# A hybrid decoder layer on one NeuronCore: the inverse's reads on SyncE's queue, and five small moves of sums, groups and input

## The chip, the cores and the metric

The kernel runs on one core of a Trainium2 chip. The metric is the device time of one execution in microseconds, as the median of several runs. The engines are TensorE (PE), VectorE (DVE), ScalarE (ACT), GpSimd (POOL) and SyncE (SP); SP only issues DMAs here.

## What is computed

One layer over 272 positions (16 learned ones ahead of 256) and 2048 features, in float32, batch 1:

```
h = layer_norm(concat([meta, x]))
p = h @ w_in                                   # columns for two head groups
y_rwkv = rwkv7_mixer(p[..., :RWKV_COLS])       # 16 heads, delta-rule state of 64x64 each
y_sb = stick_breaking_mixer(p[..., RWKV_COLS:])    # 16 heads, causal, 128-query blocks
h = layer_norm(ALPHA * h + concat([y_rwkv, y_sb]) @ w_out)
h = layer_norm(ALPHA * h + conv_ffn(h))        # gated MLP, 5632 wide, causal convolution of 3
return h[:, 16:]
```

In the first mixer every position updates the state of its head: `S = S * dec + sa (kk a)^T + v k^T` with `sa = S (-kk)`, where `kk` is the key, scaled and divided by its norm over the head, and `y = S r`. The decay and the rate `a` come from low-rank products (`w2`, `a2`), a gate from `g2`.

## The kernel before

**Weights.** All weights come in pieces of 512 KB, 128 rows by 1024 columns at a time, in the order of use. `weight` (L160) loads a piece through SP's queue (L174) into one of three raw buffers, ACT rounds it to a high half (`whi`, L183), DVE forms the difference (`wlo`, L186), and PE makes three passes over each 128 columns: high by high, high by low, low by high. `passes` (L225) and `each_pass` (L477) are these. A raw buffer is free again when DVE's difference is done, so a load waits on SP for the difference of the piece three before it.

**Order.** PE's order is the program's (`manual_schedule`, L420). The order of the instructions on every other engine, and of the DMAs in each engine's queue, is written by a planner when the program is built: it places what it believes to be ready first by durations of its own, with priorities where the program gives them (L182, L682). Each engine then takes its list in order, and waits at the head of it until that instruction's inputs are there.

**Projection and mixers.** `ORDER` names the sixteen pairs of heads, R0 to R7 for the first mixer and S0 to S7 for the second; for each the three projections are made (48 passes each), and between them, after every 16 passes (`SLOT`), `slot` gives a turn to the tasks that are due. A task is a generator that yields how many slots it waits, and how many of two small PSUM banks (`BANKS`) it needs for its next step. For each pair of the first mixer `rwkv_front` begins when k is there (key norm: squares, sums `ss` over each head by PE, root and products), and `rwkv_back` when r is there: products of two decayed factors (AG, BK), then `gram`, 36 small matmuls, masked by DVE into AG (L623), stored by POOL to a DRAM scratch `dl` (L628) and read back by POOL as LT (L631).

**The inverse.** After every second pair, `inverse` (L663) solves 36 triangular systems of 32 on POOL: 31 steps of a product (L670) and a sum (L672). POOL then stores the result to a DRAM scratch `dy` (L673) and reads it back from there with twelve DMAs into TT, with rows and columns rearranged (L678). There are four inverses, one for each two pairs of heads. `chain` (L684) walks the nine blocks of 32 positions with TT: a product with the state, copied to Wt (L701) by DVE, a product with TT (L706), a product that updates the state (L718), with 16 passes of other work between them. `rwkv_post` (L753) normalises its result (sums `gnv`, by L536 and L537).

**The head.** The input is loaded as 16 rows (256 to 271) and two tiles of 128 rows, each of these in four DMAs (L308), all on SP; statistics and normalisation are on DVE for the tiles that don't begin at row 0, on ACT for the other one (L338 to L345). In the first projections, `lora` (L391) makes the low-rank products in eight groups of two products and two sigmoids, and a tail; `proj` (L271) makes R0's v in 16 steps of three passes and yields after every second one.

**The post-norm.** After w_out, POOL adds up the tiles and their squares (`gather`, L962). The gated MLP's first products `up_step` (L1021, three passes each) start before the norm is known; after step number `MEAN` of them PE makes the two sums `p1` and `p2` (L1038), and DVE and ACT form the factors (`vv`, `rn`, `mr`), with which the first four product tiles are settled (L1045) and the tiles normalised.

Of the kernel before, what the change touches and what calls it, by code (L numbers as in the profile page):

```python
# [12 lines left out]
ALU = mybir.AluOpType  # L13
PSUM = bass.MemoryType.PSUM

P = 128
D = 2048
KT = D // P
META = 16
SEQ = 256  # L20
T = META + SEQ
# [4 lines left out]
CH = 32  # L26
# [8 lines left out]
SLOT = 16  # L35
INVERSE = 18
UNITS = 16
MEAN = 8
LATER = 8
AHEAD = 300  # L40
WARM = 42
# [8 lines left out]
RG = 3  # L50
# [63 lines left out]
def hybrid_layer(ctx, tc, xin, cst, pvec, w2a2, g2, ln2, w_in, w_out, w_up, w_down, out, dbg=None):  # L114
    nc = tc.nc
    V, S, G, PE = nc.vector, nc.scalar, nc.gpsimd, nc.tensor
# [43 lines left out]
    def weight(i, ahead=None):  # L160
        if ahead is None:
            ahead = min(5 if extra else 3, max(0, first["up"] + 3 - i) if i < first["up"] else 5)
        while len(ready) < min(len(pieces), i + ahead + 1):
            n = len(ready)
            src, m = pieces[n]
            wide = int(np.prod(src.shape)) // P
            pl, bufs = (wp, HLB)
            if extra and n % 3 == 2:
                pl, bufs = (extra[0], 2)
            if n < 4 * 3:  # L170
                raw = xw.tile([P, wide], F32, tag="xraw", bufs=4, name=f"xraw{n}")
            else:
                raw = wp.tile([P, HALF], F32, tag="wraw", bufs=RAWB, name=f"wraw{n}")
            nc.sync.dma_start(raw[:, :wide].rearrange("p (m c) -> p m c", m=m), src)  # L174
            if n < 4 * 3:
                hi, lo = [xw.tile([P, wide], F32R, tag=t, bufs=6, name=f"{t}{n}") for t in ("xhi", "xlo")]
                S.copy(hi, raw[:, :wide])
                (G if n < 3 else V).tensor_tensor(out=lo, in0=raw[:, :wide], in1=hi.bitcast(F32), op=ALU.subtract)
                ready.append((hi, lo))
                continue  # L180
            hi = pl.tile([P, HALF], F32R, tag="whi", bufs=bufs, name=f"whi{n}")
            with tc.high_priority(offset=-LATER):  # L182
                S.copy(hi[:, :wide], raw[:, :wide])  # L183
            lo = pl.tile([P, HALF], F32R, tag="wlo", bufs=bufs, name=f"wlo{n}")
            with tc.high_priority(offset=-LATER):
                V.tensor_sub(lo[:, :wide], raw[:, :wide], hi[:, :wide].bitcast(F32))  # L186
            ready.append((hi, lo))
        return ready[i]
# [36 lines left out]
    def passes(ps, hi, lo, kk, xh, xl, start, stop):  # L225
        sl = slice(kk * P, kk * P + P)
        mm(ps, lhsT=hi[:, sl], rhs=xh, start=start, stop=False)  # L227
        mm(ps, lhsT=hi[:, sl], rhs=xl, start=False, stop=False)  # L228
        mm(ps, lhsT=lo[:, sl], rhs=xh, start=False, stop=stop)  # L229
# [11 lines left out]
    ht = [htile(F32R, f"h{kt}") for kt in range(KT)]  # L241
# [26 lines left out]
        n0 = max(n0, 1)  # L268
        V.scalar_tensor_tensor(dst[:, n0:T], ps[:, n0 - 1:T - 1], mu, dst[:, n0:T], op0=ALU.mult, op1=ALU.add)  # L269

    def proj(piece, ps, n0=0):  # L271

        for hf in range(2):
            hi, lo = weight(piece + hf)
            for kk in range(8):
                kt = hf * 8 + kk
                passes(ps[:, n0:T], hi, lo, kk, ht[kt][:, 0, n0:], ht[kt][:, 1, n0:], kt == 0, kt == KT - 1)
                if kk % 2:
                    yield


    sg = []
    order = ctx.enter_context(ExitStack())
    with ExitStack() as es:
# [19 lines left out]
        for n, (a, b) in enumerate(rows):  # L304
            xt = xp.tile([P, D], F32, name=f"xt{n}")
            for k in range(4 if n else 1):
                c = slice(k * 512, k * 512 + 512) if n else slice(0, D)
                nc.sync.dma_start(xt[:b - a, c], xin[a:b, c])  # L308
            xs.append((xt, b - a, a))
        nc.sync.dma_start(cc[:, :P], cst[:, :P])  # L310
        weight(2, ahead=0)
# [5 lines left out]
        for n, (xt, r, a) in enumerate(xs):  # L317
            mv, rs, mr = [xp.tile([P, w], F32, name=f"{m}{n}") for m, w in (("mv", 2), ("rs", 1), ("mr", 1))]
# [18 lines left out]
        def normalise(k):  # L337
            c = slice(k * 512, k * 512 + 512)  # L338
            for (xt, r, a), (mv, rs, mr) in zip(xs, norm):
                if a:  # L340
                    with tc.issue_after(last.ins):
                        V.tensor_scalar(out=xt[:r, c], in0=xt[:r, c], scalar1=mv[:r, 0:1], scalar2=rs[:r],
                                        op0=ALU.subtract, op1=ALU.mult)
                else:
                    S.activation(xt[:r, c], xt[:r, c], AF.Identity, scale=rs[:r], bias=mr[:r])  # L345
# [13 lines left out]
        for kt in range(KT):  # L359
# [4 lines left out]
            for m in range(3):  # L364
                hi, lo = weight(kt // 4 * 3 + m, ahead=3)
                n0 = 12 if m else 0
# [6 lines left out]
        o = PV["mu_r"][0]  # L373
# [47 lines left out]
        low = lora()  # L421
# [3 lines left out]
        shift(acc[3], 8, k_[:, PAD:])  # L425

        val = pst.tile([P, 512], F32, tag="acc", bufs=4, name="acc4")
        for n, _ in enumerate(proj(14, val)):
            next(low, None)
        for _ in low:  # L430
            pass
        shift(val, 16, v_[:, PAD:])
        tc.keep_in_program_order(nc.scalar.preload_act_table_set("natural_log_exp_and_others"))

# [7 lines left out]
    FULL, SQUARE, HALF_COLS, QUARTER_COLS = range(4)  # L442
# [63 lines left out]
    TT = [persistent(f"TT{p}", [P, NCH, 2 * CH]) for p in range(2)]  # L506
# [51 lines left out]
    def rwkv_front(j, st):  # L558

        a = sg[j][:, 1]  # L560
        sq = atile("sq", [P, TP])
        S.activation(sq, k_, AF.Square, scale=par("k_k", j))
        sq = halves(sq, "rn", "ss")
        cum = atile("cum", [P, TP])
        V.tensor_tensor_scan(out=cum, data0=reset, data1=sg[j][:, 0], initial=0.0, op0=ALU.mult, op1=ALU.add)
        S.activation(Pt[:, :, 1:], ch(cum), AF.Exp, scale=-DECAY)
        Pinv = cum
        S.activation(Pinv, cum, AF.Exp, scale=DECAY)
        yield 2, FULL, 1
        ps = misc("ss")  # L570
        by_head(ps[:, :TP], *sq)
        ss = atile("ss", [P, TP])
        V.tensor_scalar(out=ss, in0=ps[:, :TP], scalar1=16.0, scalar2=0.5e-24, op0=ALU.mult, op1=ALU.max)
        rn = atile("rn", [P, TP])
        S.activation(rn, ss, AF.Ln, scale=2.0 * KSC)
        S.activation(rn, rn, AF.Exp, scale=-0.5, bias=lnb[:, 1:2])
        y2 = atile("sq", [P, TP])
        S.activation(y2, rn, AF.Square)
        V.tensor_mul(ss, ss, y2)
        V.scalar_tensor_tensor(rn, ss, 1.5, rn, op0=ALU.subtract, op1=ALU.mult)  # L580
        kkn = rn
        V.scalar_tensor_tensor(kkn, k_, par("k_k", j), rn, op0=ALU.mult, op1=ALU.mult)
        ba = atile("ss", [P, TP])
        V.scalar_tensor_tensor(ba, kkn, -1.0, a, op0=ALU.mult, op1=ALU.mult)
        kp = st["kp"] = atile("kp", [P, TP])
        S.activation(kp, a, AF.Identity, scale=par("k_a", j), bias=omka[:, j:j + 1])
        give(f"sg{j}")
        V.tensor_mul(kp, kp, k_)
        BK = st["BK"] = wide(f"BK{j}", n=0).rearrange("p n t -> p (n t)").rearrange("p (c x t) -> p c x t", x=2, t=CH)
        V.tensor_mul(BK[:, :, 0], ch(ba), ch(Pinv))  # L590
        V.tensor_mul(BK[:, :, 1], ch(kp), ch(Pinv))
        st["kkn"] = kkn
# [70 lines left out]
    def inverse(q, LT, Y):  # L663

        tmp = atile("ytmp", [P, NR, CH])
        n_ = RG * NB
        for s in range(CH - 1):
            n = s // RG + 1
            m = CH - 1 - s
            G.tensor_tensor(out=tmp[:n_, :n, :m], in0=Y[:n_, :n, s:s + 1].to_broadcast([n_, n, m]),  # L670
                            in1=LT[:n_, s:s + 1, s + 1:].to_broadcast([n_, n, m]), op=ALU.mult)
            G.tensor_tensor(out=Y[:n_, :n, s + 1:], in0=Y[:n_, :n, s + 1:], in1=tmp[:n_, :n, :m], op=ALU.add)  # L672
        nc.gpsimd.dma_start(dy.rearrange("b (g r) t -> g b (r t)", g=RG), Y[:n_].rearrange("p r t -> p (r t)"))  # L673
        for n in range(4):
            x, o = n % 2, n * CH
            for g in range(RG):
                k = len(range(g, CH, RG))
                nc.gpsimd.dma_start(TT[q % 2][o + g:o + CH:RG, :, CH - x * CH:2 * CH - x * CH],  # L678
                                    dy[n * NCH:n * NCH + NCH, g * NR:g * NR + k].rearrange("c r t -> r c t"))

    def first_of_all():
# [189 lines left out]
    piece = 16  # L871
    state = [dict() for _ in range(NPAIR)]
    for kind, j in ORDER:
        st = state[j]
        if kind == "R":
            for n, dst in ((1, k_), (2, v_), (0, r_)):
                if n == 0 or j:
                    ps = bank(f"R{j}{n}")
# [7 lines left out]
        else:  # L886
            qkv = []
            for n in range(3):
                n0 = Q0 if n == 0 else 0
                ps = bank(f"S{j}{n}")  # L890
# [13 lines left out]
    hs, xt = [], []  # L904
# [11 lines left out]
    for i in range(EARLY):  # L916
        ps = bank(f"o{i}")
        weave(begun(i, ps))
        hs.append(htile(F32, f"x{i}"))
        x = hs[i][:, 0, :NQ]  # L920
        hi, lo = residual(i)
# [56 lines left out]
    for i in range(EARLY):  # L978
        hi, lo = weight(wi + i // 2)
        ps = bank(f"o{i}b")  # L980
# [9 lines left out]
    for i in range(EARLY, KT):  # L990
        ps = bank(f"o{i}")
        for hf in range(2):
            hi, lo = weight(wi)
            wi += 1
            for kk in range(8):
                n = hf * 8 + kk
# [7 lines left out]
        x = hs[i][:, 0, :NQ]  # L1004
        hi, lo = residual(i)
# [85 lines left out]
    for i in range(KT):  # L1091
        x = xt[i]
# [31 lines left out]
    for f in range(4, NF):  # L1124
        pair = []
        for m in range(2):
            ps = bank(f"u{2 * f + m}")
            for hf in range(2):
                hi, lo = weight(wi)
                wi += 1  # L1130
                for kk in range(8):
                    kt = hf * 8 + kk
# [146 lines left out]
```

## Time and profile before

| | |
|---|---|
| median of 3 runs | 1409.79 us (1408.15 to 1414.41) |
| the profiled execution's own time, and its span | 1412.04 us, 1410.3 us |
| mean granted TensorE clock | 0.971 of full speed |
| busy: PE, DVE, ACT, POOL | 1336.0, 943.1, 729.5, 251.9 us |
| DMA | 223.96 MB, mean 159 GB/s |

Times in the rows below are microseconds from the start of the span. An engine's busy time is a mean over stages with different limits; what ended the idle time before an instruction stands in brackets behind it, with the length of that idle time. PEclk is the TensorE clock that was granted, as a share of full speed (2.4 GHz). SPq is SP's queue: a DMA there is shown with the time that its issue took.

### The profile page before, as it was taken

The numbers are of one execution on the slowest core, as the hardware profiler recorded it, in microseconds if no ns is written. First come the engines' busy times: TensorE is split into PE (matmuls) and PEld (weight loads), VectorE is DVE, ScalarE is ACT, GpSimd is POOL, SyncE is SP. The second block draws the span as 40 slices with busy tenths as digits, with TensorE's granted clock in tenths as the row PEclk, the third lists the DMA queues.
The fourth block names the chain that finished last, engine by engine and source line by source line (L and its number), as shares of the span: only waits on it lengthen the run. The fifth ranks groups of instructions, "written<-read, shape, count | busy, mean of one in ns | idle before, by whom it ended". The sixth has DMA issues, their size and how long they took to land.

```text
span 1410.3 us, 25107 instructions
## 1 busy us (share of the span) xinstructions
PE 1336.0 (95%) x9900; PEld 1221.5 (87%) x9900; DVE 943.1 (67%) x1546; ACT 729.5 (52%) x1263; POOL 251.9 (18%) x449
## 2 busy tenths in 40 slices
PE   8999898789999999988999999999999999999996
PEld 5988797789789889987999999999999988888895
DVE  7688577778876877798755556665656654444545
ACT  6756455457556756455644444545445443343331
POOL 4107772046172000453100000000000000000002
PEclk8999899899999999999999999999999999999999
DMA  7444433234343324543465655665655666555662
GB/s 235 133 142 130 142 117 99 84 107 140 118 126 114 113 91 154 159 145 124 152 206 162 198 189 180 193 195 184 188 183 180 185 217 214 198 186 189 198 191 94
DMA packets 68662, 223.96 MB, mean 159 GB/s; under 512 B 9912, under 2 KB 12148, under 8 KB 68400
## 3 DMA queue, kind: packets, MB, share of 16 engines
q1 hardware_dynamic: 63392, 215.03, 47.9%
q0 software_dynamic: 4288, 4.19, 1.5%
q10 hardware_dynamic: 864, 3.15, 0.6%
q8 instruction: 77, 1.26, 0.4%
q14 instruction: 41, 0.34, 0.1%
HBM read 219.01 MB, written 3.30 MB: 158 GB/s over the span
## 4 chain that ended last, share of the span: by engine, by line
PE 68%; DVE 9%; issue 3%; POOL 3%; ACT 2%; DMA 2%; POOLq 0%; DVEq 0%; ACTq 0%
PE u L1138 11%; PE u L229 6%; PE u L227 6%; PE u L228 6%; PE d L1159 6%; PE d L1158 6%; PE d L1160 6%; PE u L1139 5%; DVE wlo L186 3%; PE S L481 2%; PE S L483 2%; PE S L479 2%; ACT whi L183 1%; POOL ytmp L670 1%; POOL Y L672 1%
## 5 line engine op out<-in xcount | busy, mean ns | idle before, releaser
L186 DVE TENSOR_TENSOR wlo<-wraw,whi 128x1024 fp32r<-128x1024 f32 (+1 forms) x396 | 484.1, 1228 | 365.6 <-ACT whi L183 362.5
L183 ACT CAST whi<-wraw 128x1024 fp32r<-128x1024 f32 (+1 forms) x396 | 409.0, 1039 | 470.6 <-DMA wraw<-in_w_up_dram 143.5
L1138 PE MATMUL u<-h,whi 128*128 128x512 f32 x640 | 228.5, 398 | 0.0
L227 PE MATMUL u<-h,whi 128*128 128x258 f32 (+2 forms) x768 | 220.1, 287 | 1.9 <-ACT whi L183 1.9
L229 PE MATMUL u<-h,wlo 128*128 128x258 f32 (+2 forms) x768 | 217.9, 285 | 2.9 <-DVE wlo L186 2.9
L228 PE MATMUL u<-h,whi 128*128 128x258 f32 (+2 forms) x768 | 217.5, 284 | 0.0
L1139 PE MATMUL u<-h,wlo 128*128 128x256 f32 x640 | 180.1, 281 | 0.0
L229 PEld LDWEIGHTS u<-h,wlo 128*128 128x128 f32 x768 | 147.1, 192 | 4.0 <-DVE wlo L186 4.0
L227 PEld LDWEIGHTS u<-h,whi 128*128 128x128 f32 x768 | 146.4, 191 | 4.4 <-ACT whi L183 2.5
L228 PEld LDWEIGHTS u<-h,whi 128*128 128x128 f32 x768 | 147.1, 192 | 0.1
L1159 PE MATMUL d<-wlo,ahi 128*128 128x512 f32 (+1 forms) x396 | 145.7, 368 | 0.0
L1158 PE MATMUL d<-whi,ahi 128*128 128x512 f32 (+1 forms) x396 | 145.6, 368 | 0.0
L1160 PE MATMUL d<-whi,alo 128*128 128x512 f32 (+1 forms) x396 | 145.3, 367 | 0.0
L1138 PEld LDWEIGHTS u<-h,whi 128*128 128x128 f32 x640 | 120.6, 189 | 27.6
L1173 POOL TENSOR_TENSOR drs<-drs,mhalf 128x1 f32<-128x1 f32 x2 | 2.1, 1038 | 713.4 <-DVE drs L1172 713.4
L1139 PEld LDWEIGHTS u<-h,wlo 128*128 128x128 f32 x640 | 121.4, 190 | 0.0
L479 PE MATMUL S<-h,whi 128*128 128x272 f32 (+1 forms) x384 | 114.6, 298 | 1.6 <-DVE ql L807 1.6
L483 PE MATMUL S<-h,wlo 128*128 128x272 f32 (+1 forms) x384 | 114.7, 299 | 0.0
L481 PE MATMUL S<-h,whi 128*128 128x272 f32 (+1 forms) x384 | 114.7, 299 | 0.0
L479 PE MATMUL R<-h,whi 128*128 128x272 f32 (+1 forms) x352 | 106.3, 302 | 2.4 <-DVE shv L269 2.4
L483 PE MATMUL R<-h,wlo 128*128 128x272 f32 (+1 forms) x352 | 105.6, 300 | 0.0
L481 PE MATMUL R<-h,whi 128*128 128x272 f32 (+1 forms) x352 | 105.4, 300 | 0.0
(393 smaller groups left out, 2625.2 us busy)
## 6 DMA issues: line engine op xcount, KB each, us to landing
wraw<-in_w_up_dram SPq DMA_DIRECT2D x176, 512.0 KB, 3.9
wraw<-in_w_in_dram SPq DMA_DIRECT2D x96, 512.0 KB, 3.5
wraw<-in_w_down_dram SPq DMA_DIRECT2D x88, 512.0 KB, 4.1
wraw<-in_w_out_dram SPq DMA_DIRECT2D x28, 512.0 KB, 3.5
xraw<-in_w_in_dram SPq DMA_DIRECT2D x12, 256.0 KB, 3.8
xt<-in_xin_dram SPq DMA_DIRECT2D x8, 256.0 KB, 5.2
wraw<-in_w_out_dram SPq DMA_DIRECT2D x8, 256.0 KB, 2.5
l<-in_ln_dram ACTq DMA_DIRECT2D x1, 2048.0 KB, 8.2
```

The source lines that it names most:

```text
L183: S.copy(hi[:, :wide], raw[:, :wide])
L186: V.tensor_sub(lo[:, :wide], raw[:, :wide], hi[:, :wide].bitcast(F32))
L227: mm(ps, lhsT=hi[:, sl], rhs=xh, start=start, stop=False)
L228: mm(ps, lhsT=hi[:, sl], rhs=xl, start=False, stop=False)
L229: mm(ps, lhsT=lo[:, sl], rhs=xh, start=False, stop=stop)
L479: mm(ps, lhsT=hi[:, sl], rhs=xh, start=start, stop=False)
L481: mm(ps, lhsT=hi[:, sl], rhs=xl, start=False, stop=False)
L483: mm(ps, lhsT=lo[:, sl], rhs=xh, start=False, stop=stop)
L1138: mm(ps, lhsT=hi[:, sl], rhs=h1[:, kt, :, 2:NQ], start=kt == 0, stop=False)
L1139: mm(ps[:, :SEQ], lhsT=lo[:, sl], rhs=h1[:, kt, 0, 2:NQ], start=False, stop=kt == KT - 1)
L1158: mm(ps, lhsT=ahi[:, f, t_], rhs=hi[:, w], start=f == 0, stop=False)
L1159: mm(ps, lhsT=ahi[:, f, t_], rhs=lo[:, w], start=False, stop=False)
```

## The change

Six edits. The twelve reads of TT go into SP's queue instead of POOL's. `rwkv_front` waits three slots instead of two ahead of its sums `ss`. The post-norm's sums p1 and p2 come after `up_step` number 20 instead of 8, counted from 0. The low-rank groups come at the steps of R0's v whose number is not a multiple of three (1, 2, 4, 5, and so on) instead of behind every second step, so that the last is begun at step 11 and the tail at 13. The four DMAs of input rows 128 to 255 are issued by ACT instead of SP. The 16-row input tile is normalised by GpSimd instead of DVE.

```diff
-MEAN = 8
+MEAN = 20
...
-    def proj(piece, ps, n0=0):
-
-        for hf in range(2):
-            hi, lo = weight(piece + hf)
-            for kk in range(8):
-                kt = hf * 8 + kk
-                passes(ps[:, n0:T], hi, lo, kk, ht[kt][:, 0, n0:], ht[kt][:, 1, n0:], kt == 0, kt == KT - 1)
-                if kk % 2:
-                    yield
...
-                nc.sync.dma_start(xt[:b - a, c], xin[a:b, c])
+                (nc.scalar if a == P else nc.sync).dma_start(xt[:b - a, c], xin[a:b, c])
...
-                if a:
+                if a > P:
+                    G.tensor_scalar(out=xt[:r, c], in0=xt[:r, c], scalar1=mv[:r, 0:1], scalar2=rs[:r],
+                                    op0=ALU.subtract, op1=ALU.mult)
+                elif a:
...
-        for n, _ in enumerate(proj(14, val)):
-            next(low, None)
-        for _ in low:
-            pass
+        for kt in range(KT):
+            passes(val[:, :T], *weight(14 + kt // 8), kt % 8, ht[kt][:, 0], ht[kt][:, 1], kt == 0, kt == KT - 1)
+            if kt % 3:
+                next(low, None)
+        assert next(low, None) is None
...
-        yield 2, FULL, 1
+        yield 3, FULL, 1
         ps = misc("ss")
...
-                nc.gpsimd.dma_start(TT[q % 2][o + g:o + CH:RG, :, CH - x * CH:2 * CH - x * CH],
+                nc.sync.dma_start(TT[q % 2][o + g:o + CH:RG, :, CH - x * CH:2 * CH - x * CH],
                                     dy[n * NCH:n * NCH + NCH, g * NR:g * NR + k].rearrange("c r t -> r c t"))
```

## Rows read from the trace of the kernel before

**Rows 1.** The page: costliest groups (mean ns behind the comma), and DMA landing times.

```profile
L186 DVE TENSOR_TENSOR wlo<-wraw,whi 128x1024 fp32r<-128x1024 f32 (+1 forms) x396 | 484.1, 1228 | 365.6 <-ACT whi L183 362.5
L183 ACT CAST whi<-wraw 128x1024 fp32r<-128x1024 f32 (+1 forms) x396 | 409.0, 1039 | 470.6 <-DMA wraw<-in_w_up_dram 143.5
...
wraw<-in_w_in_dram SPq DMA_DIRECT2D x96, 512.0 KB, 3.5
```

**Rows 2.** Waits: who waited for whom, us in total, times, longest.

```profile
SPq L174 <- DVE wlo L186: 625.0, 239, 12.8
...
PE chain L706 <- DMA TT<-dy: 11.4, 4, 5.5
```

**Rows 3.** Windows: length, busy time of each engine, PEclk, DMA share, GB/s.

```profile
85.80:89.20 3.40, 3.40 (x17) 3.40 (x16) 2.65 (x6) 1.83 (x4) 0.90 (x2) 0.50 0.71 217
...
164.30:174.50 10.20, 6.47 (x33) 5.83 (x34) 1.67 (x3) 2.27 (x7) 6.65 (x12) 0.50 0.36 94
...
700.00:1390.00 690.00, 690.00 (x4306) 621.97 (x4305) 382.96 (x463) 308.49 (x409) 0.00 (x0) 1.00 0.59 189
```

**Rows 4.** POOL's timeline (start, length, instruction, idle before it) around the inverses.

```profile
154.14 0.79 POOL L673 DMA_DIRECT2D dy<-Y  x1 [0.30 <-POOL Y L672]
154.93 0.65 POOL L628 DMA_DIRECT2D dl<-AG  x1
159.97 6.98 POOL L678 DMA_DIRECT2D TT<-dy  x12 [4.40 <-DMA dy<-Y]
...
167.53 0.65 POOL L628 DMA_DIRECT2D dl<-AG  x1
...
171.63 1.25 POOL L628 DMA_DIRECT2D dl<-AG  x2
...
179.31 0.23 POOL L670 TENSOR_TENSOR ytmp<-Y,LT 108x31 f32<-108x31 f32 x1 [3.01 <-DMA LT<-dl]
...
211.17 0.79 POOL L673 DMA_DIRECT2D dy<-Y  x1 [0.30 <-POOL Y L672]
...
339.86 5.41 POOL L678 DMA_DIRECT2D TT<-dy  x9 [5.59 <-DMA dy<-Y]
...
431.10 5.84 POOL L678 DMA_DIRECT2D TT<-dy  x10 [6.26 <-PE chain L718]
```

**Rows 5.** DVE's timeline: pair 2's masks, and a difference during the first inverse.

```profile
128.15 1.39 DVE L623 TENSOR_TENSOR AG<-gram,cc 64x320 f32<-64x320 f32 x3
...
145.78 1.28 DVE L186 TENSOR_TENSOR wlo<-wraw,whi 128x1024 fp32r<-128x1024 f32 x1
```

**Rows 6.** SP's timeline: the input's issues, and one load during the first inverse.

```profile
0.73 4.19 SPq L308 DMA_DIRECT2D xt<-in_xin_dram  x9
...
133.03 0.33 SPq L174 DMA_DIRECT2D wraw<-in_w_in_dram  x1
```

**Rows 7.** PE's timeline: what it does next around each of the four inverses' ends.

```profile
149.75 1.26 PE L621 MATMUL gram<-AG,BK 64*64 64x64 f32 x36
...
166.88 0.44 PE L706 MATMUL chain<-Wt,TT 64*64 64x64 f32 x2 [5.46 <-DMA TT<-dy]
...
168.47 0.47 PE L706 MATMUL chain<-Wt,TT 64*64 64x64 f32 x2 [1.15 <-DMA TT<-dy]
...
205.79 0.33 PE L706 MATMUL chain<-Wt,TT 64*64 64x64 f32 x4
...
343.85 0.28 PE L536 MATMUL gnv<-yh,trbd 128*128 128x258 f32 x1
...
426.64 0.33 PE L706 MATMUL chain<-Wt,TT 64*64 64x64 f32 x4
```

**Rows 8.** PE's timeline: stalls ahead of the key norm's and the post-norm's sums.

```profile
84.43 0.40 PE L536 MATMUL ss<-rn,trbd 128*128 128x288 f32 x1 [1.10 <-ACT rn L530]
...
259.21 0.40 PE L536 MATMUL ss<-rn,trbd 128*128 128x288 f32 x1 [2.26 <-ACT rn L530]
...
641.72 0.79 PE L1038 MATMUL p<-s,mean 128*128 128x258 f32 x2 [2.74 <-POOL s L974]
```

## The prediction

> **What bounds the kernel now.** I read the costliest groups first. Every one of the 396 weight pieces is loaded, rounded by ACT and differenced by DVE: 3.5 us for a 512 KB load, 1039 ns for the rounding, 1228 ns for the difference [rows 1]. The waits come second: SP stands 625.0 us, 239 times, waiting for a raw buffer that DVE's difference gives back, so SP works through its list in order, one load behind the other, and PE waits 11.4 us in four stalls for TT [rows 2]. The windows come third: from 700 to 1390 us PE is busy for all 690.00 us at full clock, so that nothing before it is hidden there; every microsecond lost or won earlier reaches the end, unless a later stall takes it up. After a stall the granted clock is 0.50, the lower level, for 3.4 to 10.2 us [rows 3]. Last, the timelines of POOL, DVE, SP and PE around the four inverses [rows 4 to 7] and the stalls that the small edits aim at [rows 8].
>
> **TT's reads on SP.** The DMA that writes `dy` is issued on POOL at 154.14, the reads of it begin at 159.97 when it has landed, 5.8 us later; twelve take POOL 6.98 us, 0.58 each [rows 4]. Moving them frees POOL and makes the issue cheaper: nine issues on SP took 4.19 us, so 0.47 each [rows 6], 5.6 us for twelve (0.33 to 0.60 each as bounds: one load on SP, and POOL's own 0.58; 4.0 to 7.2). But SP's queue holds the weight loads, and a read at its head waits for `dy` with all loads behind it.
>
> So the question is where in SP's list the reads stand. Only PE's order is written by hand; the planner lists what it believes to be ready first. What it believes of the inverse shows in POOL's list: of pair 2's two `dl` stores one stands between `dy` and the reads (154.93) and one behind all reads (167.53) [rows 4], while the masks that these stores wait for were on DVE at 128.15 to 129.54 [rows 5]. So the planner takes `dy` to be written, and the reads to be ready, at about the time of those masks; on the chip that comes 25 to 30 us later, for POOL's 62 steps take 31.9 us (179.31 to 211.17) [rows 4]. I expect the reads in SP's list next to the load of 133.03 [rows 6], and at the same relative place for the other three inverses. Loads run two to three pieces ahead of PE, so a block of 25 us can't be covered.
>
> First inverse. While SP is blocked DVE has fewer differences beside POOL's steps; no row prices what they hold POOL back, I take 2.4 us (0 to 5), so `dy` has landed at some 157.6. Twelve issues: 163.2. Load 3.5, rounding 1.04, difference 1.23: 168.9. Today that difference is the one at 145.78 [rows 5], and DVE, which works in order, has pair 3's products behind it (0 to 2.7 us until gram; I take 1.4): 170.3. PE needs them for gram, which is at 149.75 today [rows 7]. Stall: **20.6**.
> Second. Pair 3's masks move with its gram: 1.26 us for it, four masks at the 0.46 of [rows 5] and a difference between them, done at 174.7. From its `dl` to the start of the inverse is 7.7 us (171.63 to 179.31), the inverse 31.9, `dy` 5.8 [rows 4]: 220.1. With 5.6 and 5.8 for issue, load and casts: 231.7, and 0.2 for the Wt copy queued behind the difference. PE wants L706 there, 205.79 today [rows 7], later by the 14.0 that the first inverse nets (20.6 less the 5.46 and 1.15 of its TT stalls): 219.8. Stall: **12.1**.
> Third and fourth, with all times moved alike: 339.86 + 5.6 + 5.8 = 351.2 against PE's gnv at 343.85: **7.4**; 431.10 + 5.6 + 5.8 = 442.5 against L706 at 426.64: **15.8** [rows 4, 7]. (The idle before 431.10 is put down to a PE product; its 6.26 us are like the 4.40 and 5.59 that `dy` costs before the other two, and I take it for `dy`.)
> Sum 55.9. Today's 11.4 for TT [rows 2] go, as PE comes later than the reads: +44.5. Half clock: the stall of 5.46 before 166.88 [rows 7] stands in a stretch of 10.2 us at 0.50 in which PE was busy 6.47, so 3.2 lost [rows 3]. Two stalls of that kind become four: +6.4 at most, 0 at least; I take +4. **TT: +48.5.** Bounds: issue at 0.33 or 0.60 gives -6.6 or +6.2 over four; if DVE's list lets PE's products pass the late difference each stall is up to 5 us shorter (-20); so +22 to +57.
>
> The Trainium skill, "DMA: Bandwidth & Descriptors", section "Issuing engine by pattern", speaks against me: it sends a simple load to Sync and calls that path generally faster, and its Specifications give about 0.6 us to the first byte there against about 1 us from GpSimd. As an estimate from that page each of the four chains of reads would gain 0.4 us, 1.6 in all, if nothing else waited; no run here shows that figure yet. It is a rule on one transfer and says nothing of what queues behind.
>
> **Key norm's sums a slot later.** PE waits 1.10 us for ACT's rounding before the sums at 84.43 and 2.26 at 259.21 [rows 8]; behind each the clock is at 0.50 for 3.4 us (85.80 to 89.20 [rows 3]; I take the same for the second), 1.7 lost each. A slot is 16 passes; 17 took 3.40 us at half clock [rows 3], so it is 1.6 us or a little more at full: it covers the first and most of the second. That is 1.1 + 1.7 + 2.26 + 1.7 = 6.8, taken as -7 with the small waits of the second product; bounds -8 to -3. The sums of the other pairs have no large wait. What follows the sums, gram included, comes up to one slot later: 0 to some +1.9 for each inverse, which PE partly had in reserve; +1.5. **-5.5.**
>
> **Post-norm's sums twelve steps later.** PE waits 2.74 at 641.72 for POOL's s [rows 8]. Twelve steps are 36 passes, by the same row 3.6 us or a little more: they fill that wait, and the half clock behind it is worth another 1.7. The sums come no sooner, POOL's s sets them; everything from vv to the settling of the first four tiles on DVE hangs on the sums, and PE would then stand before it instead. Bounds -5.3 (all kept) to +2 (the settling later); I take **-2**, nearer to nothing, because the cover behind is DVE's unchanged list.
>
> **Low-rank groups closer.** The eight groups of two products and two sigmoids come at steps 1, 2, 4, 5 and so on instead of every second one, and end some three steps sooner; what follows them waits for the shifted value from DVE, which hangs on PE's last step and not on the groups. I take **-0.8**, -1.2 to +0.5.
>
> **Input by two queues, 16 rows on POOL.** The nine issues end 4.9 us after the start [rows 6]; four on ACT's queue start those transfers up to 1.9 us sooner, but they share the DMA engines with the tile in front. **-0.7**, -1.5 to +1. GpSimd's part lies in POOL's idle time; nothing.
>
> **Sum.** 48.5 - 5.5 - 2 - 0.8 - 0.7 = +39.5. Against the profiled execution's 1412.04 us that is 1451.5; the median of the runs shown, 1409.79, lies 2.25 lower, so the time is **1449**.
>
> **Rivals.**
> (B) The reads don't block loads: the planner places them behind the loads that PE needs next, because a DMA waiting on SP is charged otherwise than one on POOL. For it: I read its beliefs from one queue only. Against it: [rows 4, 5] show it too early by 25 us on that queue, and no duration of the inverse changes. Then the first inverse's reads are issued in 5.6 instead of 6.98 us: 1.4 for each of the first two inverses, where PE waits for TT; the last two have no such stall. -2.8, with the small edits' -9.0: -11.8, so **1398**. The decision is the position of the first read against the load of 133.03: behind the load that lands last before 160, it costs nothing. The skill's rule above would have this result.
> (C) Half of it: the reads stand later in the list, or the stalls of the second and third inverse are covered by pieces already cast. Then 20.6 - 6.6 of the first is halved to some 7, the fourth leaves about 6, the second and third come out even with today's 4.8 that go: 7 + 6 - 4.8 + 1 - 9.0 = 0.2, so **1410**.
> (D) The change doesn't do what it says in its small edits: ss at a later slot meets another wait there (a bank that the transposes hold), and the -5.5 becomes 0. That adds 5.5 to the forecast, 1455, inside its range.
>
> **How the numbers follow.** Forecast (with D) 0.68: 1449, own range 1422 (TT +22, all else at -9, and the medians' offset) to 1474 (+57, small edits with D and MEAN at their worst, +7). C 0.14, spread over 1402 to 1420. B 0.18: 1390 to 1402. Half a per cent, 7 us, is about what a measurement of this kernel can tell from no change: below 1402.7 is faster, above 1416.8 slower. Faster: B 0.18 and a little of C, 0.20. Same: the middle of C, 0.10. Slower: 0.68 and the rest of C, 0.70. The range from 1400 to 1474 leaves out most of B and the top of the forecast, together 0.2.
>
> **What would show it.** In the changed profile: SP with twelve issues of 0.47 us that begin after `dy` lands, idle for 25 us or so before the first; the loads behind them in one burst; PE's longest stalls, four of 7 to 21 us, put down to DVE's difference or to DVE work behind it (AG, Wt), no longer to TT; POOL free after `dy`, with both `dl` stores of pair 2 right behind it. The stalls before ss at 84.43 and 259.21 gone, p without its wait of 2.74. Wrong I would be if the reads on SP follow loads that were issued before `dy` landed, if PE's stalls there are no longer than today, or if the difference of the late piece does not come before PE's next need on DVE.

## The result, and the profile after

The changed kernel takes 1482.74 us (median, 1480.76 to 1485.85), the kernel before 1408.97 on the same chip: 1.050 times as long, 95% interval 1.0468 to 1.0532, or some 70 us at the 1409.79 of the table. The profiled execution took 1483.41 us with a span of 1481.6. The prediction had the sign and the main mechanism, at 1449, and the time lies above its range, which ended at 1474.

Views of the changed kernel in the order in which the prediction asked for them. Its lines are numbered 7 to 10 lower in the head and 6 lower behind it; the reads of TT are L672. First what SP waits for with the reads (us in total, times, longest):

```profile
SPq L672 <- DMA dy<-Y: 91.7, 4, 28.4
```

Then SP's timeline, with all four groups of reads, and the loads behind the first:

```profile
172.36 9.87 SPq L672 DMA_DIRECT2D TT<-dy  x12
182.33 1.37 SPq L174 DMA_DIRECT2D wraw<-in_w_in_dram  x3
...
238.54 9.69 SPq L672 DMA_DIRECT2D TT<-dy  x12
...
381.13 9.76 SPq L672 DMA_DIRECT2D TT<-dy  x12
...
485.23 9.76 SPq L672 DMA_DIRECT2D TT<-dy  x12
```

And POOL's timeline at the end of the first inverse:

```profile
167.05 0.78 POOL L667 DMA_DIRECT2D dy<-Y  x1 [0.30 <-POOL Y L666]
167.84 1.25 POOL L622 DMA_DIRECT2D dl<-AG  x2
```

SP stands four times for `dy`, 91.7 us in all, with the loads behind it: after the first reads three loads leave at once at 182.33. Both `dl` stores now follow `dy` directly. In SP's list the reads stand ahead of pieces 38, 49, 73 and 91 (pieces of weights, counted from 0 in the order of use). What the prediction had expected of SP and POOL has come, except for one number: twelve issues take 9.7 to 9.9 us, not 5.6.

PE's four longest stalls, in PE's timeline, which answer [rows 7]:

```profile
187.05 0.59 PE L473 MATMUL S<-h,whi 128*128 128x272 f32 x1 [22.88 <-ACT whi L183]
...
254.90 0.47 PE L808 MATMUL vtok<-cc,sbin 128*128 128x128 f32 x1 [16.46 <-ACT sbin L889]
...
396.94 0.60 PE L473 MATMUL R<-h,whi 128*128 128x272 f32 x1 [14.45 <-ACT whi L183]
...
501.77 0.47 PE L808 MATMUL vtok<-cc,sbin 128*128 128x128 f32 x1 [12.54 <-ACT sbin L889]
```

The windows around the first two, with the columns of [rows 3]:

```profile
168.20:192.10 23.90, 4.62 (x19) 4.29 (x20) 4.96 (x6) 4.81 (x8) 3.65 (x7) 0.50 0.43 121
243.30:260.40 17.10, 5.16 (x26) 4.45 (x27) 4.74 (x10) 4.99 (x9) 0.00 (x0) 0.50 0.49 160
```

These are 66.3 us in four stalls, for ACT's rounding of the late piece or for ACT's work listed behind it; the prediction had expected DVE's difference there, or DVE's work. Around each the clock is at its lower level; the other two windows are 17.1 and 17.0 us long with PE busy for 6.10 and 7.38, so that the half clock costs half of 4.62, 5.16, 6.10 and 7.38, 11.6 us in all.

And a loss that the prediction had put at nothing, in the head, in PE's timeline:

```profile
19.29 2.50 PE L343 MATMUL tr<-cc,xt 16*128 16x16 f32 x12 [7.31 <-POOL xt L331]
21.44 1.01 PE L227 MATMUL acc<-h,xhi 128*128 128x272 f32 x3
...
30.43 0.59 PE L228 MATMUL acc<-h,xhi 128*128 128x272 f32 x1 [4.03 <-POOL h L349]
...
78.79 0.39 PE L473 MATMUL R<-h,whi 128*128 128x260 f32 x1 [2.74 <-DVE shv L269]
```

POOL's timeline, the step that the first of these waited for:

```profile
17.13 2.10 POOL L331 TENSOR_SCALAR xt<-xt,mv,rs 16x512 f32<-16x512 f32 x1
```

The same instructions in the kernel before, in PE's timeline:

```profile
12.88 2.81 PE L350 MATMUL tr<-cc,xt 16*128 16x16 f32 x12 [1.13 <-DVE xt L342]
16.16 1.03 PE L227 MATMUL acc<-h,xhi 128*128 128x272 f32 x3 [0.46 <-ACT h L351]
...
63.68 0.39 PE L479 MATMUL R<-h,whi 128*128 128x260 f32 x1 [2.38 <-DVE shv L269]
```

and in DVE's, where the 16-row step then was:

```profile
12.30 0.53 DVE L342 TENSOR_SCALAR xt<-xt,mv,rs 16x512 f32<-16x512 f32 x1
```

The first passes come 5.3 us later (16.16 to 21.44), R0's r 15.1 us later (63.68 to 78.79). PE's order is nearly the same in both kernels, so the start of the same pass in the two traces tells where the time went:

| first pass of | before | after | difference | since the line above |
|---|---|---|---|---|
| R0's r (head done) | 63.68 | 78.79 | +15.1 | +15.1 |
| piece 37 (ahead of the first late piece) | 146.76 | 159.90 | +13.1 | -2.0 |
| piece 43 | 180.18 | 212.63 | +32.5 | +19.3 |
| piece 56 | 250.87 | 296.32 | +45.5 | +13.0 |
| piece 72 | 341.73 | 379.21 | +37.5 | -8.0 |
| piece 81 | 386.25 | 440.86 | +54.6 | +17.1 |
| piece 90 | 427.81 | 487.05 | +59.2 | +4.6 |
| piece 97 | 461.19 | 536.61 | +75.4 | +16.2 |
| the MLP's passes from 693.20 on | 693.20 | 762.22 | +69.0 | -6.4 |

The rows with the four inverses give +65.6 (19.3, 13.0, 17.1, 16.2), the head +15.1, and the moved sums give some back. (In the row of +4.6 lies a stall of 2.77 us at 445.44, for DVE's `bv`; the later `ss` alone brings one like it.)

### The profile page after: what moved, and what is told of

It reads as the page before. It is cut to its first block, busy times and chain, and to the rows that moved or that the text cites. A ratio compares the mean times of both kernels' runs of the same rounds, so it can differ in the third digit from the quotient of the medians.

```text
span 1481.6 us, 25115 instructions
## 1 busy us (share of the span) xinstructions
PE 1339.2 (90%) x9900; PEld 1223.3 (83%) x9900; DVE 938.3 (63%) x1542; ACT 726.9 (49%) x1263; POOL 231.4 (16%) x405
## 3 DMA queue, kind: packets, MB, share of 16 engines
q1 hardware_dynamic: 67936, 214.57, 45.5%
## 4 chain that ended last, share of the span: by engine, by line
PE 46%; DMA 10%; DVE 9%; issue 4%; ACT 4%; POOL 2%; SPq 1%; POOLq 0%; DVEq 0%; ACTq 0%
PE u L1132 10%; DMA wraw<-in_w_down_dram 9%; PE u L229 6%; PE u L227 6%; PE u L228 6%; PE u L1133 5%; DVE wlo L186 4%; ACT whi L183 3%; PE S L475 2%; PE S L477 2%; PE S L473 2%; SPq L672 1%; POOL ytmp L664 1%; POOL Y L666 1%; PE o L473 1%
## 5 line engine op out<-in xcount | busy, mean ns | idle before, releaser
L473 PE MATMUL R<-h,whi 128*128 128x272 f32 (+1 forms) x352 | 105.8, 301 | 17.2 <-ACT whi L183 14.5
```

## The experiments

Each ran beside the kernel before on the same chip; the ratios are to that, with their 95% intervals, and in us at 1409.79.

**tt_only**: the kernel before with one line changed.

```diff
-                nc.gpsimd.dma_start(TT[q % 2][o + g:o + CH:RG, :, CH - x * CH:2 * CH - x * CH],
+                nc.sync.dma_start(TT[q % 2][o + g:o + CH:RG, :, CH - x * CH:2 * CH - x * CH],
```

> The kernel before, with TT's twelve reads in SP's queue and nothing else changed. Theory (the reads stand in SP's list ahead of loads that PE needs, and SP stands there until the inverse is done): in the changed kernel PE's four long stalls are 22.9, 16.5, 14.5 and 12.5 us, 66 in all, 11.4 of TT stalls are gone; so about +58 to +66 over the kernel before, 1467 to 1475, with four stalls of that size. Rival (the loss comes from the other five edits and their combination): under +30.

1.0450 (1.0411 to 1.0488), +63 us. PE's four stalls:

```profile
171.90 0.59 PE L479 MATMUL S<-h,whi 128*128 128x272 f32 x1 [20.61 <-ACT whi L183]
...
240.71 0.37 PE L718 MATMUL chain<-R,BT 64*64 64x64 f32 x2 [18.38 <-DVE R L711]
...
383.93 0.58 PE L536 MATMUL gnv<-yh,trbd 128*128 128x258 f32 x1 [11.80 <-ACT yh L530]
...
487.70 0.47 PE L814 MATMUL vtok<-cc,sbin 128*128 128x128 f32 x1 [15.35 <-ACT sbin L895]
```

One edit makes nine tenths of the loss, by four stalls of 66.1 us in all. The reads stand ahead of pieces 38, 50, 73 and 91.

**rest_only**: the changed kernel with that line back on `nc.gpsimd`.

> The changed kernel with TT's reads back in POOL's queue: the other five edits together. By the passes' times in the changed kernel the head costs +15 to +16.6, the later sums of the key norm give back some 3 to 11, the post-norm's sums some 6. Theory: the sum is about nothing, 1400 to 1414, with PE's stalls of 7.3 and 4.0 us near 19 and 30 us still there. Rival (the head's loss is taken up by the first inverse, which PE waits for in any case): below 1398.

0.9975 (0.9957 to 0.9993), -3.5 us, within the theory. The head's stalls are there (6.32 and 4.28 us), R0's r starts 14.9 us late; the first inverse doesn't take up the head's loss, and PE waits longer for TT than before, 7.99 instead of the 5.46 of [rows 7].

**tt_late**: the reads on SP, but traced behind a later load and ahead of the chain's first step.

```diff
+LATEST = (-1, -1, -3, -1)
+EARLIER = (4, 1, 1, 1)
...
+    def reads(q):
...
-                nc.gpsimd.dma_start(TT[q % 2][o + g:o + CH:RG, :, CH - x * CH:2 * CH - x * CH],
-                                    dy[n * NCH:n * NCH + NCH, g * NR:g * NR + k].rearrange("c r t -> r c t"))
+                nc.sync.dma_start(TT[q % 2][o + g:o + CH:RG, :, CH - x * CH:2 * CH - x * CH],
+                                  dy[n * NCH:n * NCH + NCH, g * NR:g * NR + k].rearrange("c r t -> r c t"))
...
-        yield INVERSE, QUARTER_COLS, 0
+        yield INVERSE - EARLIER[q], QUARTER_COLS, 0
+        with first_of_all(), tc.issue_after(loads[LATEST[q]]):
+            reads(q)
+        yield EARLIER[q], QUARTER_COLS, 0
```

> The kernel before, with TT's reads in SP's queue, but listed behind the loads that are issued by the time the inverse is done (ahead of pieces 46, 54, 76 and 96 instead of 38, 50, 73 and 91). Theory (the place in the list makes the price): none of the four long stalls; the reads end later than on POOL, by 0.82 instead of 0.58 us an issue and, for the first inverse, by waiting behind a load, so TT stalls of some 13 and 6 us instead of 6.6 and 4.9: +5 to +12, 1414 to 1421. Rival (reads of TT on SP are slow by themselves, or their transfers in that queue hold up the loads): +30 or more.

1.0036 (1.0018 to 1.0053), +5 us, at the lower end of the theory's range. In the kernel that ran the first reads stand ahead of piece 41, not 46 as the text above has it; the other three are as told. SP waited 22.5 us for `dy` in all, 14.3 in the longest of four times. SP's timeline at the first reads:

```profile
159.74 9.86 SPq L683 DMA_DIRECT2D TT<-dy  x12
169.71 1.55 SPq L176 DMA_DIRECT2D wraw<-in_w_in_dram  x3
```

and PE's, with its two stalls for TT, of 5.4 and 4.7 us where the text above has 13 and 6:

```profile
167.26 0.44 PE L714 MATMUL chain<-Wt,TT 64*64 64x64 f32 x2 [5.44 <-DMA TT<-dy]
172.39 0.45 PE L714 MATMUL chain<-Wt,TT 64*64 64x64 f32 x2 [4.69 <-DMA TT<-dy]
```

So the same reads on the same queue cost 5 us instead of 63 with other places in the list. SP still stands 14.3 us for the first `dy`, but the pieces held up, 41 and later, are not wanted before PE waits for TT in any case. The second stall, 4.69 where [rows 7] have 1.15, goes mostly with the slower issue: the last read is issued at 169.6 instead of 167.0. By the starts of the same passes, the first inverse loses 5.6 us in this way (pieces 40 to 42), and the second gives as much back, as PE has no stall for TT there any more. What stays comes at the third: the reads, issued from 338.55 to 348.64, hold up three loads, the next masks stand in DVE's list behind the difference of the first of these pieces, and PE waits 4.49 us for them at 355.91.

**tt_nowait**: the reads on SP come from a scratch `dz`, written once ahead of the first inverse, and the chains compute with those values.

```diff
+    dz = dp.tile([NB, NR * RG, CH], F32, name="dz")
...
+        if q == 0:
+            nc.gpsimd.dma_start(dz.rearrange("b (g r) t -> g b (r t)", g=RG), Y[:n_].rearrange("p r t -> p (r t)"))
...
-                nc.gpsimd.dma_start(TT[q % 2][o + g:o + CH:RG, :, CH - x * CH:2 * CH - x * CH],
-                                    dy[n * NCH:n * NCH + NCH, g * NR:g * NR + k].rearrange("c r t -> r c t"))
+                nc.sync.dma_start(TT[q % 2][o + g:o + CH:RG, :, CH - x * CH:2 * CH - x * CH],
+                                    dz[n * NCH:n * NCH + NCH, g * NR:g * NR + k].rearrange("c r t -> r c t"))
```

> The kernel before, with TT's reads in SP's queue, but from a scratch that is written once ahead of the first inverse and not by the inverses, so that nothing waits for them (the chains then compute with those values instead of the inverse's). Theory (it is the wait at the head of SP's queue): 48 issues of 0.82 us, in bursts of at most 9.8 us that two or three pieces ahead cover, no stall over 5 us from them, and the TT stalls of 11.4 us with their half clock gone: 1392 to 1406. Rival (the issues and transfers themselves hold up the loads): no faster than before, 1410 to 1440.

0.9908 (0.9873 to 0.9942), -13 us. With the wait gone, 48 reads in SP's queue are covered by the pieces ahead, and what is left fits the gain of having no TT stall and no half clock behind one. So neither SP's path nor the transfers cost the 63 us. The places are not those of tt_only, though: with nothing to wait for, the planner lists the reads earlier, in groups of one to five between the loads from piece 22 on, the first at 73.89. That the wait does the harm at the places of tt_only follows from this run, the 91.7 us that SP waits for `dy` in the changed kernel, and tt_late together.

**norm_pool**: the 16-row tile on GpSimd alone.

```diff
-                if a:
+                if a > P:
+                    G.tensor_scalar(out=xt[:r, c], in0=xt[:r, c], scalar1=mv[:r, 0:1], scalar2=rs[:r],
+                                    op0=ALU.subtract, op1=ALU.mult)
+                elif a:
```

> The kernel before, with the 16-row tile normalised by GpSimd and nothing else changed. Theory (a 16x512 step that took DVE 0.53 us takes GpSimd about 2 us, and PE's first transposes and ACT's and POOL's steps behind them wait for it): the first passes begin 3 to 4 us later, POOL's tiles h come later too, +8 to +14 by the third stage of the head, part of it taken up by the first inverse's stalls: 1.003 to 1.010 of the time before. Rival (the head's loss is the input's two queues): 0.999 to 1.002.

1.0052 (1.0031 to 1.0073), +7 us. POOL's timeline:

```profile
12.56 8.28 POOL L341 TENSOR_SCALAR xt<-xt,mv,rs 16x512 f32<-16x512 f32 x4
20.82 0.54 POOL L332 TENSOR_TENSOR rs<-rs,mhalf 128x1 f32<-128x1 f32 x1
```

DVE's, at the normalisation that needs that root:

```profile
21.39 4.76 DVE L345 TENSOR_SCALAR xt<-xt,mv,rs 128x512 f32<-128x512 f32 x4 [8.57 <-POOL rs L332]
```

A step that took DVE 0.53 us takes POOL 2.07. The four stand in POOL's list ahead of the root of the third tile's variance, and DVE stands 8.57 us for that. PE's first passes start at 24.07, 7.9 us later, twice the 3 to 4 of the theory, and R0's r at 71.82, 8.1 us later.

**norm_pool_rs**: the same, with the four steps listed behind that root.

```diff
-            G.tensor_tensor(out=rs[:r], in0=rs[:r], in1=mhalf[:r], op=ALU.pow)
+            root = G.tensor_tensor(out=rs[:r], in0=rs[:r], in1=mhalf[:r], op=ALU.pow)
...
+                if a > P:
+                    with tc.issue_after(root.ins):
+                        G.tensor_scalar(out=xt[:r, c], in0=xt[:r, c], scalar1=mv[:r, 0:1], scalar2=rs[:r],
+                                        op0=ALU.subtract, op1=ALU.mult)
```

> The kernel before, with the 16-row tile normalised by GpSimd, but with these steps listed behind the root of the third tile's variance on POOL (0.54 us) instead of ahead of it. Theory (what costs 7.9 us at the first passes is that this root stands behind four steps of 2.07 us, and DVE's normalisation of the third tile with it): first passes +1 to +4 instead of +7.9. Rival (PE's first transposes wait for the four steps themselves): +7 or more.

1.0025 (1.0004 to 1.0046), +3.5 us, and the first passes at 18.55, 2.4 later than before: the theory. So the larger part of the 7.9 at the first passes was the place in POOL's list. At R0's r less is won: it starts at 69.30, 5.6 us later than before, against 8.1 in norm_pool. The four steps still take POOL some 9 us, and now hold up POOL's differences of the first weights, for which PE waits:

```profile
24.86 0.58 PE L229 MATMUL acc<-h,xlo 128*128 128x260 f32 x1 [2.05 <-POOL xlo L178]
```

That the kernel as a whole is better for the new place, +3.5 instead of +7, the two intervals, which overlap, don't show.

**input_2q**: rows 128 to 255 issued by ACT, alone.

```diff
-                nc.sync.dma_start(xt[:b - a, c], xin[a:b, c])
+                (nc.scalar if a == P else nc.sync).dma_start(xt[:b - a, c], xin[a:b, c])
```

> The kernel before, with rows 128 to 255 of the input issued by ACT and nothing else changed. Theory (the transfers share the DMA engines, so the tile of rows 0 to 127, whose statistics come first, lands later and the other one no sooner): DVE's statistics end 1 to 1.5 us later, first passes +1 to +2: 1.000 to 1.002. Rival (as forecast in the prediction): first passes 0.7 us sooner, 0.999 to 1.000. Second rival (this edit is what costs the head its 15 us): first passes +4 or more.

1.0055 (1.0034 to 1.0077), +8 us, with the first passes 6.7 us later, as the second rival has it; of the head's 15 us this is half (R0's r at 71.06, +7.4). The page's DMA issues, from issue to landing by queue (KB each, median us):

```profile
xt<-in_xin_dram ACTq DMA_DIRECT2D x4, 256.0 KB, 6.3
xt<-in_xin_dram SPq DMA_DIRECT2D x4, 256.0 KB, 7.4
```

DVE's timeline at the statistics:

```profile
9.56 3.66 DVE L322 BATCH_NORM_STATS2 st<-xt 128x6 f32<-128x512 f32 x6 [2.83 <-DMA xt<-in_xin_dram]
```

PE's at the first transposes and passes:

```profile
20.71 2.50 PE L350 MATMUL tr<-cc,xt 16*128 16x16 f32 x12 [7.57 <-DVE xt L342]
22.86 1.01 PE L227 MATMUL acc<-h,xhi 128*128 128x272 f32 x3
```

Before, the eight transfers took 5.2 us (median; 5.2 to 6.6 over the runs that leave the input on SP), one tile behind the other. Now the two tiles land together, rows 0 to 127 at 11.4 us instead of 6.9: DVE's six remaining statistics wait until 9.56 and run as one block, with both aggregates behind them. They end 1.3 us later than before, as I had expected. But POOL's roots come behind both aggregates now, that of the 16 rows last, so that DVE's first step on these rows, at 12.30 before, starts at 16.73; and it takes 3.92 us instead of 0.53, during the same time in which POOL makes three differences:

```profile
16.73 3.92 DVE L342 TENSOR_SCALAR xt<-xt,mv,rs 16x512 f32<-16x512 f32 x1 [1.02 <-POOL rs L332]
```

```profile
16.68 3.69 POOL L178 TENSOR_TENSOR xlo<-xraw,xhi 128x512 fp32r<-128x512 f32 x3
```

These two, 4.4 us of a later root and 3.4 us of a longer step, are the 7.8 us by which the first transposes come later (12.88 to 20.71). That the step is long because POOL works beside it is a reading; no run was made to show it.

**ss_only**: `yield 3, FULL, 1` for `yield 2, FULL, 1` ahead of `ss`.

> The kernel before, with the key norm's sums one slot later and nothing else changed. By the changed kernel's pass times: the waits before the sums go (1.10 and 2.26 us, with half clock), but new waits of 2.1 to 2.3 us stand before the bonus sums, for DVE's masks, at the first pairs. Theory: -4 to -9, 0.9935 to 0.997. Rival (what the first four pairs win is taken up by PE's wait for the first inverse, and only the later pairs count): -1 to -4.

0.9926 (0.9906 to 0.9947), -10.4 us, just beyond the theory. No `ss` waits any more; the new waits before the bonus sums are there, and PE waits for TT 3.6 us longer at the first inverse and 3.5 shorter at the second, so that these two cancel. In PE's timeline:

```profile
105.35 0.56 PE L536 MATMUL bonus<-rkh,trbd 128*128 128x258 f32 x1 [2.12 <-DVE AG L623]
...
166.59 0.44 PE L706 MATMUL chain<-Wt,TT 64*64 64x64 f32 x2 [7.80 <-DMA TT<-dy]
169.41 0.44 PE L706 MATMUL chain<-Wt,TT 64*64 64x64 f32 x2 [2.38 <-DMA TT<-dy]
...
226.29 0.30 PE L706 MATMUL chain<-Wt,TT 64*64 64x64 f32 x2 [1.38 <-DMA TT<-dy]
```

By the starts of the same passes, 3.7 us are won from R0's r to piece 37 and 6.7 between pieces 54 and 60. In this second stretch the kernel before has, beside the 2.26 us ahead of `ss` [rows 8], a wait that is gone too, with a stretch of 6.8 us at half clock around it:

```profile
271.86 0.32 PE L736 MATMUL y<-AG,R 128*64 128x32 f32 x2 [2.34 <-DVE BT L661]
```

**mean_only**: `MEAN = 20`.

> The kernel before, with the post-norm's sums after step 20 instead of 8 and nothing else changed. Theory (the stalls of 0.87 and 2.74 us and the half clock behind them are filled with passes, and the sums come no later): -4.5 to -6.5, 0.9953 to 0.997. Rival (as the prediction has it, most of it is taken up where the first four tiles are settled): -1 to -3.

0.9958 (0.9940 to 0.9976), -5.9 us: the theory. In PE's timeline the four products run without a wait, at the time at which the last two ran before [rows 8]:

```profile
641.93 1.03 PE L1038 MATMUL p<-s,mean 128*128 128x258 f32 x4
```

**low_only**: the low-rank groups at the steps not divisible by three.

> The kernel before, with the low-rank groups closer and nothing else changed. Theory: PE's stall behind them is for the shifted value and stays at some 2.4 us, as in the changed kernel (2.74); 0.999 to 1.001. Rival (the prediction's -0.8 to -1.2): 0.999 or less.

0.9989 (0.9965 to 1.0014): no difference that can be told. The stall ahead of R0's r is 2.74 us, for DVE's shifted value as before (2.38).

**ss_mean_low** and **ss_mean**: the edits that help, with the low-rank one and without.

> The kernel before with three edits: the key norm's sums one slot later, the post-norm's sums after step 20, the low-rank groups closer. Alone the first gave -10.5 us and the second -6.9 us in the passes' times. Theory: they lie in different stages and add up, and the low-rank edit is worth -1 to +1: -14 to -19, 0.9865 to 0.9905. Rival (they share what PE has to wait for behind them): -10 or less.

> The same without the low-rank edit. Theory: within 1.5 us of the kernel with all three, either way; -14 to -18. Rival (the prediction's -0.8 for the low-rank groups, or more): slower than the kernel with all three by 0.8 us or more.

0.9873 (0.9842 to 0.9904) and 0.9865 (0.9830 to 0.9900), -18 and -19 us: the two edits add up (-16 by the sum, within the intervals), and the low-rank edit makes no difference here either. **ss_mean**, 1394.59 us (median, 1391.43 to 1398.61), is faster than both kernels.

## Why the prediction was wrong

The change costs some 70 us instead of the 39.5 forecast, 31 more. By the runs of single edits, TT's reads are 15 of these and the head 16; the key norm's and the post-norm's sums give 9 back; and some 10 arise only where TT's reads and the other edits meet.

**Right: where the reads stand, and that PE stalls for the loads behind them.** The reads were to stand next to the load of 133.03, which is piece 38; they stand right ahead of it. What PE waits for is not what was forecast: ACT's rounding or work listed behind it, and in tt_only once DVE's R, but never the difference. The first inverse is 2.3 us shorter (130.77 to 167.05, 36.3 us; before 115.55 to 154.14, 38.6), for 2.4 assumed; the prediction had no row for that, so this is luck. Half clock was to cost 10.4 (the 6.4 of today and 4 more) and cost 11.6.

| inverse | stall forecast | tt_only | changed kernel |
|---|---|---|---|
| first | 20.6 | 20.61 | 22.88 |
| second | 12.1 | 18.38 | 16.46 |
| third | 7.4 | 11.80 | 14.45 |
| fourth | 15.8 | 15.35 | 12.54 |
| sum | 55.9 | 66.1 | 66.3 |

That the first stall of tt_only is as forecast is luck too: the late piece is ready 1.6 us later than forecast (171.90 instead of 170.3), and PE goes on as much longer, as it stops only for the late piece itself and not for gram. (In the second, the 0.2 of the Wt copy is counted twice; 11.9 would be the sum.)

**Wrong: the price of an issue.** "0.47 each, 5.6 us for twelve (0.33 to 0.60 as bounds)" came from DMAs of long rows. One read of TT gathers 11x9 (or 10x9) pieces of 32 numbers, and its issue (ns min/median/max, first and last start) is on POOL's queue in the kernel before:

```profile
L678 POOL DMA_DIRECT2D TT<-dy x48: 579/589/628, 160.0 to 439.0; - x48
```

and on SP's in the changed one:

```profile
L672 SPq DMA_DIRECT2D TT<-dy x48: 750/762/950, 172.4 to 494.2; - x48
```

Twelve take 9.87 instead of 5.6, 4.3 more in each inverse and 17 in all, beyond the upper bound. At the first inverse part of it was won back behind the reads: from the end of the issues to PE I had 7.2 us, and it is 4.8 (182.23 to 187.05), as PE's first pass needs only the high half, and gram's products were listed ahead. At the other three it is 6.0 to 6.8, for 5.8. The term was +48.5 with bounds to +57; alone it is +63 (58 to 69 by its interval): the stalls are 66.1 for 55.9, 10 of the 14.5 us that the term was short, and the rest is within the interval. Which property of the gather makes its issue longer, no run tells. The Trainium skill ("DMA: Bandwidth & Descriptors", "Issuing engine by pattern") calls Sync's path generally faster; for the issue of this gather the trace says the opposite, 762 against 589 ns, and the measurement decides. Rival B, which stood on a free place in the list, is near to what tt_late built. It comes to +5, not -2.8: the slower issue costs the first inverse what the second gives back, and at the third the reads still hold up loads.

**Wrong: the head.** "GpSimd's part lies in POOL's idle time; nothing", and -0.7 for the input. They are +7 and +8 alone (+8.1 and +7.4 at R0's r), and +15.1 together at R0's r. For the first, the idle time was there, but the step's duration on POOL had no row and I gave it no bound, and I did not ask what is listed behind it on POOL, nor that PE's very first transposes need its result. The Trainium skill ("GPSIMD Engine Reference", "Engine selection") has one-input elementwise work on GpSimd at roughly line rate; 2.07 against DVE's 0.53 us is four times. For the input I counted the issue that starts sooner and not the tile that it delays, nor what comes behind that in the lists of POOL and DVE.

**Too small: the two sums.** The key norm's sums were put at -5.5 and give -10.4. The +1.5 for later inverses did not come in the sum, as the waits for TT at the first two cancel, and the wait ahead of `y` at 271.86 goes with its half clock, for which there was no term. The post-norm's were put at -2, on the argument that the settling would take up the gain; nothing took it up, -5.9, just beyond the bound of -5.3. The low-rank -0.8 is not to be told from nothing.

**Not additive.** The six edits alone sum to 63 + 7 + 8 - 10 - 6 - 2 = +60, together they are +70. The five without TT's do add up (-3 by the sum, -3.5 measured), so the 10 lie between them and TT's reads. The starts of the same passes, in us behind the kernel before, tell where:

| first pass of | tt_only | rest_only | changed kernel |
|---|---|---|---|
| piece 50 | 34.6 | 17.4 | 51.8 |
| piece 52 | 29.1 | 12.5 | 47.1 |
| piece 72 | 28.1 | 2.5 | 37.5 |
| piece 74 | 42.1 | 2.2 | 56.2 |

As far as piece 50 the two add up. From there to piece 52 each of the three makes up some 5 us, for the TT stalls of the second inverse that the kernel before has there: they can go only once, and that is half of the 10. Most of the other half arises at the third inverse, from piece 72 to 74 (14.0 us in tt_only, 18.7 in the changed kernel). POOL's steps there take 34.1 us, against 32.2 in tt_only; what makes them longer, and the rest, is open.

## What to carry to other kernels

Before a waiting DMA is put on a queue, find out where in that queue's list it will stand and what is behind it: the planner lists by its own durations, and the order of a neighbouring queue shows what it believes. A wait is free only if everything behind it is wanted later than the wait ends: the same reads cost +63 us ahead of pieces 38, 50, 73 and 91 and +5 ahead of 41, 54, 76 and 96. And idle time of an engine is not a price of nothing: a step that moves to it needs a duration of its own there, and a look at the instructions behind it.

## What the runs showed of the hardware

The issue of a DMA depends on its shape and on the queue: 0.33 us for a weight load on SP [rows 6], 0.76 for a gather of 11x9x32 there, 0.59 for the same gather on POOL. A 16x512 subtract and multiply in float32 takes DVE 0.53 us and GpSimd 2.07. But DVE's took 3.92 us once in input_2q, beside three of GpSimd's differences, and in the kernel before two of four took 1.5, beside the same. And in DVE's timeline of norm_pool_rs two of four small steps, all beside GpSimd's long ones, took 1.24 us and the other two 0.16:

```profile
16.41 1.24 DVE L378 TENSOR_SCALAR omu<-pv 128x27 f32<-128x27 f32 x1
17.56 0.16 DVE L381 TENSOR_SCALAR ngn<-pv 128x8 f32<-128x8 f32 x1
17.63 1.24 DVE L381 TENSOR_SCALAR nsb<-pv 128x8 f32<-128x8 f32 x1
18.78 0.16 DVE L383 TENSOR_SCALAR omka<-pv 128x8 f32<-128x8 f32 x1
```

That DVE's steps waited for GpSimd there is my reading; no run was made to show it.
